# The SWA output and mix projections as one plain pair and three pairs of seven products

## The chip, the cores and the metric

The kernel runs on one core of one Trainium2 chip. The metric is the device time of one execution in microseconds (us). It is measured in several runs and given as their median; a profiled execution of the same program gives the durations of single instructions. Engines are named as the profile names them: PE is TensorE (matmuls), PEld its weight loads, DVE is VectorE, ACT is ScalarE, POOL is GpSimd, SP is SyncE, which issues nearly all DMAs here.

## What is computed

One step of a one-layer streaming encoder on 1024 prompt tokens and 64 sample tokens, 1088 columns in all, with a model width of 1024. The part that matters here merges two branches and adds the result to the input, after which cross-attention normalises it:

```python
def merge_branches(ret_o, ret_g, swa_o, gate_a, gate_b, w_ret_out, w_swa_out, w_mix_out):
    B, S = ret_g.shape[:2]
    a = (rms_norm(ret_o).astype(ret_g.dtype).reshape(B, S, -1) * jax.nn.silu(ret_g)) @ w_ret_out
    b = swa_o.reshape(B, S, -1) @ w_swa_out
    return (jax.nn.sigmoid(gate_a) * a + jax.nn.sigmoid(gate_b) * b) @ w_mix_out
...
x += merge_branches(...)
x += CrossAttn(RMSNorm(x), memory K/V)
x += SwiGLU(RMSNorm(x))
```

`w_swa_out` and `w_mix_out` are 1024 x 1024 each.

## The kernel before

Activations are kept transposed: feature rows on the 128 partitions (eight row tiles, k or m = 0 to 7), tokens along the free dimension. A full-precision product is made of three matmuls of rounded halves: `split` (line 122) copies a tile to a rounded high part on ACT and subtracts it on DVE for the low part, and high times high, high times low and low times high are summed in PSUM.

There are two ways to project. The dense way (`dense`, line 153) takes one weight tile row `m` against eight k and a chunk of 384, 384 or 320 columns (`CH`); `m_major` (line 1042) orders rows and chunks. The seven-product way (`strassen`, line 247) cuts a pair of weight rows, `m` and `m + 4`, and the activations into 2 x 2 quarters and makes seven products where a plain scheme (`plain`, line 225) makes eight. The quarters are 4 row tiles by half of the columns (`HALF` = 544, in two PSUM banks of 272), called B11, B12, B21 and B22, and the seven products need four differences of them, T1 to T4, as operands too. The weight sums are formed by four operations on POOL (`weight_ops`, line 166), and seven weight splits follow for a pair. Before the change the first projections, the FFN's gate and up and its down projection use seven products; the SWA output, the mix, the cross-attention and the retention output projections use the dense way.

SBUF holds two rings of eight large slots each (`Ring`, line 100), which stages take over from one another; a slot is written when its last reader is done. Scratch in DRAM (`d_swa`, `d_gate`, `d_mix`, `d_h`, `d_op`) carries results between stages. Pools hand out tiles in rotation, so a load waits for the buffer that it overwrites. PSUM has eight banks.

The stages around the change are these. `mix_phase` (line 843) runs the sliding-window attention; between its steps, PE gets pieces of the retention output projection (`filler`, line 1053), of which eight pieces remain after the last step, and whose gated results go to `d_mix`. The attention's tiles lie in ring 0, the retention operands in ring 1. At the end of `mix_phase` stands `merge_swa` (line 1101). It loads `d_swa` chunk by chunk, splits it into ring 0, projects with `w_swa_out`, multiplies by the gate (line 1121), adds `d_mix` (line 1122) and splits the result into ring 1, all on DVE and ACT. It then projects with `w_mix_out`, adds the input (line 1130), stores `d_h`, forms the gained and split operand `xc` of the next stage (`gained`, line 265) and sums the squares; as soon as a column chunk is complete its root is formed (`to_rstd`, line 309), through `later`, which runs after the next dense projection. `cross_phase` (line 1139) then projects `xc` with `w_cq`, in order of k, and scales by the roots.

The order of instructions on each engine is that of a scheduler which simulates the program by priorities; each engine and each DMA queue then runs its instructions in that order.

Of the kernel before, what the change touches and what calls it, by code (L numbers as in the profile page):

```python
# [109 lines left out]
class Kernel:  # L110
# [86 lines left out]
    def multiply(self, ps, w, xs, first=True, last=True):  # L197

        mm = self.nc.tensor.matmul
        for k, x in enumerate(xs):  # L200
            ks = slice(k * P, (k + 1) * P)
            start, stop = first and k == 0, last and k == len(xs) - 1
# [22 lines left out]
    def plain(self, w, x, emit, early=None):  # L225
# [19 lines left out]
        emit(1, 1, part(1, 1, 1), None)  # L245

# [86 lines left out]
    def run(self):  # L333
        nc, tc, io = self.nc, self.tc, self.io
        with ExitStack() as ctx:
# [34 lines left out]
            with ExitStack() as sctx:  # L370
# [472 lines left out]
    def mix_phase(self):  # L843
# [17 lines left out]
        self.merge_swa()  # L861
# [239 lines left out]
    def merge_swa(self):  # L1101
        nc, tc, io = self.nc, self.tc, self.io
        with ExitStack() as ctx:
            bp = ctx.enter_context(tc.tile_pool(name="bq", bufs=2, reuse_waits="tile"))
            pn = ctx.enter_context(tc.tile_pool(name="pnb", bufs=1, reuse_waits="tile", space=PSUM))
            self.norm_psum = lambda name: pn.tile([P, 512], F32, tag="n", name=name)
            ld = lambda: bp.tile([P, 384], F32, tag="ld", bufs=8, name="ld")
            unit = lambda w: [lambda m=m: self.unit(io[w][m], KT) for m in range(KT)]
            swas = self.ring_tiles(0, KT, "swa")
            for c0, n in CH:  # L1110
                for k in range(KT):
                    a = ld()
                    self.load(a[:, :n], self.d_swa[k, :, c0:c0 + n])
                    self.split(a[:, :n], swas[k][:, 0, c0:c0 + n], swas[k][:, 1, c0:c0 + n])
            mixs = self.ring_tiles(1, KT, "mix")
            for m, u, (c0, n) in self.m_major(unit("w_swa_out"), CH, lead=2):
                g, a = ld(), ld()
                self.load(g[:, :n], self.d_gate[2][m, :, c0:c0 + n])
                self.load(a[:, :n], self.d_mix[m, :, c0:c0 + n])
                ps = self.dense(u, swas, c0, n)  # L1120
                nc.vector.tensor_tensor(out=g[:, :n], in0=ps, in1=g[:, :n], op=ALU.mult)
                nc.vector.tensor_tensor(out=a[:, :n], in0=a[:, :n], in1=g[:, :n], op=ALU.add)
                self.split(a[:, :n], mixs[m][:, 0, c0:c0 + n], mixs[m][:, 1, c0:c0 + n])
            self.xs = self.ring_tiles(0, KT, "xc")
            for m, u, (c0, n) in self.m_major(unit("w_mix_out"), CH):
                x = ld()
                self.load(x[:, :n], io["xT"][m, :, c0:c0 + n])
                ps = self.dense(u, mixs, c0, n)
                x = x[:, :n]
                nc.vector.tensor_tensor(out=x, in0=ps, in1=x, op=ALU.add)  # L1130
                self.store(self.d_h[0][m, :, c0:c0 + n], x)
                acc = self.rstd[:, c0:c0 + n]
                self.gained(self.xs[m], c0, n, x, self.gains[:, 1, :], m)
                self.add_square(acc, x, m == 0, bp, n)
                if m == KT - 1:
                    root = self.root[:, c0 // 384, :]
                    self.later.append(lambda acc=acc, root=root: self.to_rstd(acc, acc, root=root))
# [559 lines left out]
```

## Time and profile before

| What | Value |
|---|---|
| median of 3 runs | 2241.72 us (2241.03 to 2244.38) |
| profiled execution, its own time | 2239.58 us |
| its span in the profile | 2237.8 us |
| SWA output projection in it | 1035.0 to 1130.5 us |
| mix projection in it | 1130.5 to 1227.2 us |
| mean granted PE clock | 0.986 |

Times in the profile count from the start of the span. A row of a group reads: line, engine, operation, output<-inputs by tile name, shapes, number of instructions, then busy time in us and mean ns of one, then idle time of the engine just before them and who ended it. A row of waits reads: the engine and instruction that waited, the one it waited for, then us in total, times, and the longest. A row of the timeline reads: start, duration, engine, line, operation.

### The profile page before, as it was taken

Reading aid. Unit: us, or ns where it says so; the run is one execution under the profiler, and the core shown is the slowest. Engines: PE = TensorE matmul, PEld = TensorE weight load, DVE = VectorE, ACT = ScalarE, POOL = GpSimd, SP = SyncE. Lnnn points to the kernel's source line nnn. Section 1 sums busy time; section 2 is a strip of 40 time slices with the busy share of each in tenths; the row PEclk is TensorE's granted clock in tenths of the full one; section 3 lists DMA queues with packets and bytes.
Section 4 is the critical chain, followed back from the end, with each engine's and each line's share of the span. In section 5 each row is a group of like instructions: output and inputs, shape, how many; then the busy total and the mean of one; then the engine's idle time right before and its main releaser. Section 6 shows DMA issues by size and latency. Waiting matters only on the chain.

```text
span 2237.8 us, 41757 instructions
## 1 busy us (share of the span) xinstructions
PE 2171.3 (97%) x16434; PEld 2106.8 (94%) x16434; DVE 1600.4 (72%) x2655; ACT 884.7 (40%) x1897; POOL 690.5 (31%) x466
## 2 busy tenths in 40 slices
PE   9999999999999989999999999999999999999996
PEld 9899999999999977779999998999999999999986
DVE  8986878676687668876455555668777777778588
ACT  7333333435444355553133333333222222334243
POOL 1441533342253112220000000014555555434462
PEclk9999999999999999999999999999999999999998
DMA  5433345443445475326443112422332332475233
GB/s 205 156 111 110 117 123 137 133 127 113 167 152 178 151 229 169 114 75 208 130 154 107 55 48 65 134 85 88 122 130 101 102 122 89 142 273 182 84 102 109
DMA packets 182599, 290.86 MB, mean 130 GB/s; under 512 B 40290, under 2 KB 110850, under 8 KB 182402
## 3 DMA queue, kind: packets, MB, share of 16 engines
q1 hardware_dynamic: 177794, 279.26, 39.3%
q10 hardware_dynamic: 4608, 8.91, 1.1%
q8 instruction: 130, 2.13, 0.4%
q14 instruction: 67, 0.55, 0.1%
HBM read 196.95 MB, written 91.16 MB: 129 GB/s over the span
## 4 chain that ended last, share of the span: by engine, by line
PE 75%; DVE 7%; DMA 4%; issue 1%; ACT 1%; POOL 1%; SPq 0%; DVEq 0%; ACTq 0%; POOLq 0%
PE pq L208 14%; PE pq L206 14%; PE pq L205 14%; PE pd L149 7%; PE pd L151 7%; PE pd L150 7%; PE pout L1000 1%; DMA hl<-d_op 1%; PE pp L984 1%; DVE wq L124 1%; PE pss L942 1%; DMA ld<-d_swa 1%; DVE B L124 1%; DMA raw<-w_ret_out 1%; PE pk L699 0%
## 5 line engine op out<-in xcount | busy, mean ns | idle before, releaser
L124 DVE TENSOR_TENSOR wq<-raw,wq 128x512 fp32r<-128x512 f32 (+1 forms) x505 | 450.1, 895 | 124.8 <-ACT wq L123 122.6
L123 ACT CAST wq<-raw 128x512 fp32r<-128x512 f32 (+1 forms) x505 | 307.6, 614 | 569.9 <-PE pq L208 262.7
L205 PE MATMUL pq<-T,wq 128*128 128x272 f32 x1832 | 493.9, 289 | 6.2 <-DVE u L252 3.6
L206 PE MATMUL pq<-T,wq 128*128 128x272 f32 x1832 | 493.9, 289 | 0.0
L206 PE MATMUL pq<-B,wq 128*128 128x272 f32 x1592 | 429.3, 289 | 8.4 <-DVE B L124 8.4
L205 PE MATMUL pq<-B,wq 128*128 128x272 f32 x1592 | 426.7, 288 | 0.0
L208 PE MATMUL pq<-T,wq 128*128 128x272 f32 x1832 | 384.4, 290 | 3.4 <-DVE wq L124 3.4
L183 POOL TENSOR_TENSOR raw<-raw 128x512 f32<-128x512 f32 (+1 forms) x59 | 79.4, 1345 | 894.8 <-DVE rs_r L291 483.8
L205 PEld LDWEIGHTS pq<-T,wq 128*128 128x128 f32 x1832 | 346.7, 189 | 7.1 <-DVE u L252 3.7
L206 PEld LDWEIGHTS pq<-T,wq 128*128 128x128 f32 x1832 | 346.8, 189 | 0.3 <-issue 0.3
L208 PE MATMUL pq<-B,wq 128*128 128x272 f32 x1592 | 334.0, 290 | 0.0
L206 PEld LDWEIGHTS pq<-B,wq 128*128 128x128 f32 x1592 | 300.7, 189 | 10.3 <-DVE B L124 10.0
L205 PEld LDWEIGHTS pq<-B,wq 128*128 128x128 f32 x1592 | 300.1, 189 | 0.7 <-issue 0.4
L208 PEld LDWEIGHTS pq<-T,wq 128*128 128x128 f32 x1832 | 292.0, 191 | 4.6 <-DVE wq L124 3.8
L208 PEld LDWEIGHTS pq<-B,wq 128*128 128x128 f32 x1592 | 253.5, 190 | 0.5 <-issue 0.3
L252 DVE TENSOR_TENSOR u<-pq,u 128x544 f32<-128x544 f32 x177 | 127.5, 720 | 111.7 <-PE pq L208 111.1
L186 POOL TENSOR_TENSOR raw<-raw 128x512 f32<-128x512 f32 (+1 forms) x59 | 85.3, 1446 | 125.2 <-DVE wq L124 122.6
L970 POOL TENSOR_TENSOR t<-t,den 128x768 f32<-128x768 f32 (+2 forms) x34 | 47.8, 1406 | 167.7 <-DVE den L968 49.9
L571 DVE TENSOR_TENSOR stage<-pq,u 128x544 f32<-128x544 f32 x112 | 80.3, 717 | 26.6 <-PE pq L208 25.8
L184 POOL TENSOR_TENSOR raw<-raw 128x512 f32<-128x512 f32 (+1 forms) x59 | 89.2, 1512 | 3.7
L1455 POOL TENSOR_TENSOR y<-u,y 128x544 f32<-128x544 f32 x38 | 62.6, 1658 | 72.4 <-DVE y L1453 54.4
L189 POOL TENSOR_TENSOR raw<-raw 128x512 f32<-128x512 f32 (+1 forms) x59 | 83.2, 1411 | 4.4
(373 smaller groups left out, 4674.2 us busy)
## 6 DMA issues: line engine op xcount, KB each, us to landing
hl<-d_op SPq DMA_DIRECT2D x85, 272.0 KB, 4.4
d_qkv<-stage SPq DMA_DIRECT2D x44, 272.0 KB, 2.3
d_op<-stage SPq DMA_DIRECT2D x44, 272.0 KB, 2.1
d_op<-ht SPq DMA_DIRECT2D x44, 272.0 KB, 3.3
raw<-w_gate SPq DMA_DIRECT2D x22, 512.0 KB, 3.5
raw<-w_up SPq DMA_DIRECT2D x22, 512.0 KB, 3.6
d_gate<-stage ACTq DMA_DIRECT2D x32, 272.0 KB, 2.8
raw<-w_down SPq DMA_DIRECT2D x16, 512.0 KB, 4.4
```

The lines of the kernel that those rows point to most:

```text
L123: self.last_cast = self.nc.scalar.copy(hi, src).ins
L124: return self.nc.vector.tensor_tensor(out=lo, in0=src, in1=hi.bitcast(F32), op=ALU.subtract).ins
L149: mm(ps, wh, xh, start=start, stop=False)
L150: mm(ps, wh, xl, start=False, stop=False)
L151: self.last_mm = mm(ps, wl, xh, start=False, stop=stop).ins
L184: tt(out=a21, in0=a21, in1=a22, op=add)
L186: tt(out=a11, in0=a22, in1=a11, op=sub)
L189: tt(out=a12, in0=a12, in1=a11, op=sub)
L205: mm(ps[:, c, :HC], w[:, 0, ks], x[:, 0, cs], start=start, stop=False)
L206: mm(ps[:, c, :HC], w[:, 0, ks], x[:, 1, cs], start=False, stop=False)
L208: self.last_mm = mm(ps[:, c, :HC], w[:, 1, ks], x[:, 0, c * HC:(c + 1) * HC], start=False, stop=stop).ins
L252: add = lambda out, a, b: nc.vector.tensor_tensor(out=out, in0=a, in1=b, op=ALU.add)
```

## The change

`merge_swa` is written anew, and it is called after `mix_phase` with PSUM to itself: `plain_psum` is closed before it and opened again, on the right side, for `cross_phase`; the memory tiles' pool is closed before it too.

- Both projections work on pairs of rows `n` and `n + 4`. Pair 0 is made plain (eight products, `quarters_in_parts`), pairs 1 to 3 with seven products each.
- The quarters of `d_swa` are loaded (16 tiles of 128 x 544) and split, the 16 differences T1 to T4 are formed in place on POOL and split. The slots are given by hand (`place`): B operands in ring 0, in the order in which the attention leaves its tiles, T operands in ring 1.
- The gated result of a pair is multiplied on DVE; the addition of `d_mix` is on POOL for pairs 0 to 2 and on DVE for pair 3; the differences of the results are formed on POOL. Most of them are stored to `d_op` and loaded again as the mix projection's operands: B12, B21 and B22 as the last pair's products free slots (`refill`), T1 to T4 after the first plain pair. Of B11 the pairs 1 and 2, and of all quarters pair 3, are split directly.
- In the mix projection's plain pair the products run over the first three k of all quarters, and then over the fourth.
- For pairs 1 to 3 of the mix projection the side sum is added to the input on POOL, and the PSUM part on DVE. `xc` is formed directly for pair 3; rows 0, 4, 1, 5, 2, 6 are loaded again from `d_h` as slots come free. The squares are summed per half of the columns.
- The roots of all three column chunks are formed through `later` in `cross_phase`, whose dense projections go over k in the order 0, 4, 1, 5, 2, 6, 3, 7.

```diff
-    def multiply(self, ps, w, xs, first=True, last=True):
+    def multiply(self, ps, w, xs, first=True, last=True, tiles=None):
...
+    def quarters_in_parts(self, w, x, emit, parts):
...
+        ps, left = {}, {}
+        for i, t, j, ks in parts:
+            left[i, t] = left.get((i, t), 0) + len(ks)
+        for i, t, j, ks in parts:
+            first = (i, t) not in ps
+            if first:
+                ps[i, t] = self.bank_pair()
+            left[i, t] -= len(ks)
+            out = self.multiply(ps[i, t], w[i, j], x[f"B{j + 1}{t + 1}"], first, not left[i, t], ks)
+            if not left[i, t]:
+                emit(i, t, out, None)
...
-                    with self.plain_psum():
+                    with self.plain_psum(side="right"):
                         self.mix_phase()
-                        self.mem.close()
+                    self.mem.close()
+                    self.merge_swa()
+                    with self.plain_psum(side="right"):
                         self.cross_phase()
...
+            self.fp = ctx.enter_context(tc.tile_pool(name="fm", bufs=1, reuse_waits="tile"))
+            left = ctx.enter_context(tc.tile_pool(name="ml", bufs=10, reuse_waits="tile"))
+            right = ctx.enter_context(tc.tile_pool(name="mr", bufs=8, reuse_waits="tile", side="right"))
+            self.ps = ctx.enter_context(tc.tile_pool(name="psm", bufs=4, reuse_waits="tile", space=PSUM))
...
+            for k in range(4):
+                b11, b12, b21, b22 = (raw[name, k] for name in ("B11", "B12", "B21", "B22"))
+                for out, x, y in ((b11, b12, b11), (b12, b22, b12), (b22, b22, b11), (b21, b21, b22)):
+                    nc.gpsimd.tensor_tensor(out=out, in0=x, in1=y, op=sub)
+                for name, x in (("T2", b22), ("T1", b11), ("T3", b12), ("T4", b21)):
+                    put(ops, name, k, x)
...
+                    g, a = fetch(self.d_gate[2][m, :, half(t)]), fetch(self.d_mix[m, :, half(t)])
+                    o = g
+                    if sb is None:
+                        tt(out=banks(o), in0=ps, in1=banks(g), op=ALU.mult)
+                    else:
+                        o = st()
+                        tt(out=banks(o), in0=ps, in1=sb, op=ALU.add)
+                        tt(out=o, in0=o, in1=g, op=ALU.mult)
+                    (nc.vector if last else nc.gpsimd).tensor_tensor(out=o, in0=o, in1=a, op=ALU.add)
+                    h[i, t], spare[i, t] = o, a
+                    name = quarter[i, t]
+                    if last or (name == "B11" and n):
+                        put(mixs, name, n, o)
+                    else:
+                        self.store(saved(name, n), o)
+                    for name, at, x, y in (("T1", (0, 0), (0, 1), (0, 0)), ("T2", (1, 1), (1, 1), "T1"),
+                                           ("T3", (0, 1), (1, 1), (0, 1)), ("T4", (1, 0), (1, 0), "T2")):
+                        if name not in h and x in h and y in h:
+                            h[name] = spare[at]
+                            nc.gpsimd.tensor_tensor(out=h[name], in0=h[x], in1=h[y], op=sub)
+                            self.store(saved(name, n), h[name])
...
+            self.quarters_in_parts(first, ops, gated(0), [(i, t, j, all4) for t in range(2) for j in range(2) for i in range(2)])
...
+            def refill(name):
+                new = {"B11": "B12", "B21": "B21", "T2": "B22"}.get(name)
+                if new:
+                    begin(mixs, places, new, place[name])
+                    for k in three:
+                        put(mixs, new, k, fetch(saved(new, k)))
...
+                    x = fetch(io["xT"][m, :, half(t)])
+                    if sb is not None:
+                        nc.gpsimd.tensor_tensor(out=banks(x), in0=banks(x), in1=sb, op=ALU.add)
+                    tt(out=banks(x), in0=ps, in1=banks(x), op=ALU.add)
+                    self.store(self.d_h[0][m, :, half(t)], x)
+                    if n == 3:
+                        gain(m, t, x)
...
+            for name, old in (("T2", "B22"), ("T1", "T1"), ("T3", "T3"), ("T4", "T4")):
+                begin(mixs, places, name, place[old])
+                for k in all4:
+                    put(mixs, name, k, fetch(saved(name, k)))
...
+            def norms(i=0):
+                c0, n = CH[i]
                 acc = self.rstd[:, c0:c0 + n]
...
+                self.to_rstd(acc, acc, root=self.root[:, i, :])
+                if i < 2:
+                    self.later.append(lambda: norms(i + 1))
...
+            order = (0, 4, 1, 5, 2, 6, 3, 7)
+            xs = [self.xs[k] for k in order]
```

More of the change, by code (lines that the diff above doesn't have):

```diff
@@ L1106, in merge_swa @@
[L1106 to L1123, printed above, removed]
@@ new lines, in fetch @@
+            def fetch(src):
+                a = st()
+                self.load(a, src)
+                return a
+            ring = lambda r, *slots: (r, [(self.rings[r].next + i) % KT for i in slots])
+            place = {"B11": ring(0, 5, 7), "B21": ring(0, 2, 1), "B12": ring(0, 0, 4), "B22": ring(0, 3, 6),
+                     "T1": ring(1, 0, 1), "T2": ring(1, 2, 3), "T3": ring(1, 4, 5), "T4": ring(1, 6, 7)}
+            pair = lambda w, n: self.load_raws([io[w][n], io[w][n + 4]])
+            saved = lambda name, k: self.d_op[OPS.index(name), k]
@@ L1172, in attend @@
                 for c0, n in CQ:
-                    ps = [self.dense(us[i], self.xs, c0, n) for i in range(2)]
+                    ps = [self.dense(us[i], xs, c0, n) for i in range(2)]
                     qf = t2("qf")
```

105 lines of the change are left out of this document (84 added, 21 removed).

## The prediction

> **What bounds the kernel now.** I read first the page's busy shares and its chain of waits.
>
> ```profile
> span 2237.8 us, 41757 instructions
> ...
> PE 2171.3 (97%) x16434; PEld 2106.8 (94%) x16434; DVE 1600.4 (72%) x2655; ACT 884.7 (40%) x1897; POOL 690.5 (31%) x466
> ...
> PE 75%; DVE 7%; DMA 4%; issue 1%; ACT 1%; POOL 1%; SPq 0%; DVEq 0%; ACTq 0%; POOLq 0%
> ```
>
> TensorE sets the end, so fewer matmuls shorten the kernel as long as nothing else in the stage takes over. Next, the view by stretches (columns: length, then busy time and instruction count of PE, PEld, DVE, ACT, POOL; clock; DMA share; GB/s): the two projections, then two stretches of the FFN, which already uses the seven-product form.
>
> ```profile
> 1035.00:1130.50 95.50, 95.29 (x579) 94.85 (x578) 54.04 (x102) 27.73 (x54) 0.00 (x0) 1.00 0.56 169
> 1130.50:1227.20 96.70, 96.70 (x596) 96.70 (x595) 48.84 (x98) 34.92 (x67) 0.00 (x0) 1.00 0.39 125
> 1600.00:1700.00 100.00, 100.00 (x805) 100.00 (x805) 72.75 (x88) 29.77 (x50) 55.43 (x38) 1.00 0.33 112
> 1920.00:2000.00 80.00, 78.27 (x627) 77.84 (x626) 63.55 (x86) 34.19 (x59) 26.60 (x17) 1.00 0.74 256
> ```
>
> The view of the tiles `swa` and `mix` puts the borders of the stages there:
>
> ```profile
> L149 PE MATMUL pd<-swa,wq x192: 306/334/442, 1035.2 to 1130.2; 128*128 128x384 f32 x128, 128*128 128x320 f32 x64
> L149 PE MATMUL pd<-mix,wq x192: 306/334/423, 1130.6 to 1226.9; 128*128 128x384 f32 x128, 128*128 128x320 f32 x64
> ```
>
> and TensorE's waits from 1015 to 1235 us are one:
>
> ```profile
> PE pd L149 <- ACT swa L123: 0.2, 1, 0.2
> ```
>
> So the old stage costs 95.5 + 96.7 = 192.2 us, all matmul, with GpSimd wholly idle and VectorE about half busy. A new loss there cannot replace an old wait: there is none.
>
> **Part 1, products removed.** In the FFN 805 matmuls of 272 columns take 100 us, 0.1242 us each; a product (4 k, 6 matmuls) is 24 of them, 2.98 us. The wide matmuls do 24 x 8 x 1088 columns in 95.5 us, 0.457 ns a column, and 272 of those are 0.1243 us: the narrow form loses nothing. Each projection goes from 32 products to 8 + 3 x 7 = 29: 86.4 us. Both: 192.2 - 172.8 = 19.4 us less PE work. The 1.2 us between the two stages is norm matmuls (596 instructions against 579) that only move behind the stage.
>
> **Part 2, what VectorE and GpSimd are given.** Prices, from the groups by form of 1035:1227 (first fence) and 1520:1920 (second), and the views of single lines (third: min/median/max ns):
>
> ```profile
> L124 DVE TENSOR_TENSOR wq<-raw,wq 128x512 fp32r<-128x512 f32 x33 | 22.8, 691 | 4.9 <-ACT wq L123 4.2
> ...
> L269 DVE SCALAR_TENSOR_TENSOR xc<-ld,gains,xc 128x384 fp32r<-128x384 f32 x16 | 9.9, 619 | 11.0 <-ACT xc L268 11.0
> ...
> L269 DVE SCALAR_TENSOR_TENSOR xc<-ld,gains,xc 128x320 fp32r<-128x320 f32 x7 | 3.8, 546 | 0.0
> ```
> ```profile
> L124 DVE TENSOR_TENSOR wq<-raw,wq 128x512 fp32r<-128x512 f32 x134 | 143.5, 1072 | 37.3 <-ACT wq L123 37.0
> ...
> L252 DVE TENSOR_TENSOR u<-pq,u 128x544 f32<-128x544 f32 x57 | 41.2, 723 | 48.6 <-PE pq L208 48.4
> ```
> ```profile
> L1388 POOL TENSOR_TENSOR ht<-stage x10: 1364/1372/1375, 1544.5 to 1919.6; 128x544 f32<-128x544 f32 x10
> ...
> L1388 DVE TENSOR_TENSOR ht<-stage x1: 716/716/716, 1977.4 to 1977.4; 128x544 f32<-128x544 f32 x1
> ```
> ```profile
> L183 POOL TENSOR_TENSOR raw<-raw x59: 1013/1295/2607, 20.4 to 2179.6; 128x512 f32<-128x512 f32 x55, 128x384 f32<-128x384 f32 x4
> ```
>
> The same weight split takes 691 ns while GpSimd is idle and 1072 where it works. The timeline of VectorE and of GpSimd around 1641 us says why:
>
> ```profile
> 1641.15 1.19 DVE L124 TENSOR_TENSOR wq<-raw,wq 128x512 fp32r<-128x512 f32 x1 [0.70 <-ACT wq L123]
> 1642.72 0.72 DVE L252 TENSOR_TENSOR u<-pq,u 128x544 f32<-128x544 f32 x1 [0.37 <-PE pq L208]
> ```
> ```profile
> 1640.43 1.37 POOL L1373 TENSOR_TENSOR stage<-stage,rstd_f 128x544 f32<-128x544 f32 x1
> 1641.75 1.75 POOL L184 TENSOR_TENSOR raw<-raw 128x512 f32<-128x512 f32 x1
> ```
>
> The split starts at 1641.15 and ends at 1642.34, 0.54 us after the GpSimd operation before it (1641.80): it waited and then ran. The GpSimd operation that starts meanwhile needs 1.75 us where 1.295 is usual: it waited for the split. The two take turns, with some 0.69 - 0.54 = 0.15 us of overlap per GpSimd operation. An add that reads PSUM (L252) runs beside GpSimd at its usual 0.72. The Trainium skill, page "SBUF — State Buffer", section "Who interferes with whom", calls this an exclusive lock between GpSimd and a VectorE operation with two SBUF inputs, one side fully blocked; the trace agrees but for that overlap, and without it the sum below would be some 11 us larger. It is a rule that speaks against this change.
>
> So I add what needs its turn. A VectorE operation with two SBUF inputs costs 0.717 (544 columns) or 0.691 (512), a gain 0.80 (0.619 plus 160 columns at the 73 ns per 64 between its two forms), GpSimd 1.364 or 1.295, less 0.14 per GpSimd operation.
>
> SWA projection, GpSimd: 16 differences of `swa`, 12 gated adds, 16 differences of `mix` (44 x 1.364 = 60.0) and 12 weight sums (15.5): 75.5. VectorE: 32 operand splits (22.9), 29 weight splits (20.0), 12 products by the gate and 4 last adds (11.5), 16 operand splits of `mix` (11.5): 66. Sum 141.5, less 56 x 0.14: 133.7 us.
>
> Mix projection, GpSimd: 12 weight sums and 12 adds, 31.9. VectorE: 16 splits of saved differences (11.5), 25 weight splits (17.3), 14 square sums (10.0), 16 gains (12.8): 51.6. Sum 83.5, less 24 x 0.14: 80.1 us.
>
> **Part 3, what of it is done early.** The last store of `d_swa`, and the last store out of the attention's spare buffers (tile view, SyncE's timeline):
>
> ```profile
> L120 SPq DMA_DIRECT2D d_swa<-osb x9: 370/371/386, 858.1 to 1020.4; - x9
> ```
> ```profile
> 1037.87 0.38 SPq L120 DMA_DIRECT2D d_mix<-swin  x1
> ```
>
> The first half's columns are stored well before, so B11 and B21 (8 splits, 5.7) and four weight splits (2.8) fit before 1035; of the second half, which loads after 1020.4, four B12 splits and four differences (2.9 + 4.9). B22's slots are those spare buffers, read until after 1038. Early: 16.3 us. Left: 133.7 - 16.3 + 80.1 = 197.5 us of turns against 172.8 of matmul. The turns, not TensorE, set this stage. All of it is needed: operands and weights by TensorE, adds and saved differences within a rotation of 18 buffers, so little of it can be put off; some 12 us of the first projection slip into the second, which is itself over (92 against 86.4). Bounds: 172.8, if turns cost nothing, to 197.5 / 0.88 = 224, if they are used only as far as the FFN does (16 GpSimd and 22 VectorE operations per 41.7 us pair, 36.6 us by these prices, 88%, with TensorE never waiting there). I take 197.5 + 3: queues in order, casts on ScalarE before each split, and a slower clock after a wait, as here:
>
> ```profile
> 1514.06 0.93 PE L330 MATMUL pb<-ident,rs_r 128*128 128x128 f32 x6 [2.05 <-ACT rstd_f L331]
> ...
> 1515.90 0.43 PE L206 MATMUL pq<-b,wq 128*128 128x272 f32 x1
> 1516.12 0.43 PE L205 MATMUL pq<-b,wq 128*128 128x272 f32 x1
> ...
> 1518.93 0.29 PE L206 MATMUL pq<-b,wq 128*128 128x272 f32 x1
> ```
>
> (0.22 us apart instead of 0.12 for 3 us, worth 1.4 us.)
>
> **Part 4, the end.** The norms now start after the last product: add 0.72, square 0.66, sum 0.72, then the steps that stand in the timeline before, pt to the root:
>
> ```profile
> 1221.68 0.72 PE L306 MATMUL pt<-ones,rstd 128*128 128x2 f32 x6
> ...
> 1224.43 0.15 DVE L294 SCALAR_TENSOR_TENSOR rs_r<-rs_t,rs_r 128x3 f32<-128x3 f32 x1
> ```
>
> 2.9, then spread and copy 1.3: about 6.3. TensorE has three projections of 256 columns to do meanwhile (24 x 0.117 = 2.8 each, three banks), and the order of k puts the last column tile last. Bounds 0 to 5, I take 2, plus the 1.2 of moved matmuls.
>
> **Part 5, DMA.** Quarter tiles are 272 KB (0.279 MB). First projection: about 10 `d_swa`, 32 gate and mix, 26 saves, 10 reloads, 8 weights: 26 MB, 270 to 300 GB/s over 86 to 97 us. All go through SyncE, where a load that waits for its buffer holds those behind it. The FFN's turn ran 256 GB/s at a share of 0.74, about 346 at full. I take 0; if the burst at the turn (last pair and next plain pair: 45 quarter tiles and 4 weights, 14.6 MB in 44.7 us) ran at 300, 4 us.
>
> **The sum.** 197.5 + 3 + 2 + 1.2 - 192.2 = +11.5 us. On the profiled execution (2239.6, span 2237.8) that is 2251.1; the median of the runs is 2.1 higher: 2253.
>
> **Rivals.**
> A. The turns are hidden. By engine alone the first projection needs 75.5 on GpSimd and 66 + 18 PSUM operations (12.9) = 79 on VectorE, both under 86.4. For it: in 1600:1700 both engines sum to 128 of 100 us while TensorE never waits. Against: that stage fills at most 88% of its time with turns, this one 114% (197.5 of 172.8). It needs early or put-off work of 25 us. Left are 2 at the start, the FFN's turn,
>
> ```profile
> PE pq L206 <- DVE B L124: 4.8, 5, 1.3
> ```
>
> and 3.2 at the end: -19.4 + 2 + 4.8 + 3.2 = -9.4, 2232.
> B. VectorE blocked by GpSimd frees PSUM late and TensorE's waits idle the turns again, so these are used only 88%: 224 + 3.2 - 192.2 = +35, 2277. It decides once the gated adds queue on GpSimd ahead of the next weights (12 GpSimd operations in the 20.9 us of a pair, 16 us at least). For: strict order on both. Against: four PSUM pairs give some slack.
> C. As A, with DMA late at the turn by 4 us: 2237.
>
> **How the numbers follow.** Forecast 0.50 (2245 to 2267), A 0.26, B 0.17, C 0.07. A run tells a change of 0.2%, 4.5 us. Faster: A, 0.26. Same: C and the low end of the forecast, 0.11. Slower: 0.63. For 8 in 10 the range takes in A and B: 2226 to 2281.
>
> **What would show it.** Matmuls of the stage about 1390 (two times 29 x 24) at 0.124; the stage lasting 197 to 205 us instead of 192; splits of `wq` there about 1.07 instead of 0.69 and GpSimd differences at 1.5 to 1.8; TensorE waiting for VectorE's operand and weight splits from the first seven-product pair on; the later stages unchanged. Wrong: TensorE without waits in the pairs, or long waits on loads.

## The result, and the profile after

The changed kernel takes 2277.13 us (median of 6 runs, 2275.40 to 2281.79) against 2241.49 us of the kernel before (6 runs beside it): a ratio of 1.0156, 95% interval 1.0143 to 1.0170. It is slower by 35.6 us, where 11.5 were forecast. The time lies inside the range, at its upper end, and nearest to rival B (2277).

The page of the profile after, the lines that stand against those of before:

```profile
span 2274.7 us, 42432 instructions
...
PE 2167.3 (95%) x16674; PEld 2100.4 (92%) x16674; DVE 1687.1 (74%) x2668; ACT 913.3 (40%) x1923; POOL 826.3 (36%) x546
...
PE 66%; DVE 10%; DMA 6%; issue 3%; POOL 2%; ACT 1%; SPq 0%; DVEq 0%; POOLq 0%; ACTq 0%
```

TensorE's work fell by 4 us, but its share of the chain fell from 75% to 66%; DVE, DMA and POOL took it. The view of TensorE's waits from 1018 to 1290 us, where before one wait of 0.2 us stood:

```profile
PE pd L149 <- DVE st L1232: 14.3, 1, 14.3
PE pq L206 <- DVE st L1232: 5.0, 3, 4.4
PE pq L207 <- DVE B L124: 4.4, 2, 4.1
PE pq L206 <- DVE u L268: 4.4, 1, 4.4
PE pq L206 <- ACT T L123: 3.7, 1, 3.7
PE pq L206 <- DVE st L1182: 3.0, 1, 3.0
PE pq L209 <- DVE wq L124: 1.7, 1, 1.7
PE pq L206 <- DVE st L1185: 1.1, 1, 1.1
PE pq L206 <- ACT u L271: 1.1, 2, 0.9
```

The wait of 14.3 us stands at the end of the stage, ahead of the first `w_cq` matmul; the others lie among the products and sum to 24.4 us. The view by stretches (columns as in the prediction) shows where:

```profile
1035.00:1060.00 25.00, 22.33 (x176) 22.11 (x175) 24.61 (x20) 14.21 (x24) 19.44 (x11) 1.00 0.43 157
1060.00:1085.00 25.00, 18.52 (x103) 17.69 (x104) 25.00 (x21) 7.20 (x13) 22.86 (x14) 0.73 0.38 119
1085.00:1110.00 25.00, 25.00 (x202) 25.00 (x202) 21.61 (x23) 5.74 (x11) 20.15 (x13) 1.00 0.75 237
...
1135.00:1147.40 12.40, 7.99 (x54) 7.77 (x53) 11.29 (x15) 4.85 (x9) 3.27 (x2) 0.86 0.99 344
...
1172.00:1197.00 25.00, 17.28 (x108) 17.06 (x109) 18.37 (x25) 14.10 (x23) 4.75 (x3) 0.80 0.69 243
1197.00:1222.00 25.00, 25.00 (x203) 25.00 (x202) 19.20 (x23) 7.71 (x13) 15.07 (x10) 1.00 0.55 191
...
1248.90:1263.20 14.30, 0.03 (x1) 0.06 (x1) 10.65 (x14) 6.52 (x11) 4.20 (x3) 0.62 0.61 198
```

The matmuls of the products carry their times in the trace, so each block of 24 gives one product; whatever it lasts beyond 2.98 us is its loss. The first matmul is at 1037.6, the first of `w_cq` at 1263.2: 225.6 us for the stage, against 192.2 before. Of this, 58 products are 172.8. The losses, with the products counted from 1:

| Where | Loss, us |
|---|---|
| products 7, 8 and 11 (end of the plain pair, start of the next) | 6.05 + 1.72 + 7.43 = 15.2 |
| products 24, 25, 27 and 28 (last SWA pair) | 1.39 + 0.29 + 0.43 + 6.00 = 8.1 |
| products 38 and 40 (turn from the mix projection's plain pair to the next) | 6.74 + 5.23 = 12.0 |
| products 54, 55 and 58 | 2.4 |
| the wait ahead of the first `w_cq` matmul | 14.3 |

They sum to 52.0; the last 0.8 us is spread. The products' losses (37.7) are larger than their waits (24.4), mostly because TensorE runs at half pace after a long wait. After the first one:

```profile
1061.41 0.60 PE L207 MATMUL pq<-B,wq 128*128 128x272 f32 x1 [4.08 <-DVE B L124]
1061.80 0.43 PE L206 MATMUL pq<-B,wq 128*128 128x272 f32 x1
...
1067.51 0.43 PE L206 MATMUL pq<-B,wq 128*128 128x272 f32 x1
...
1068.52 0.29 PE L206 MATMUL pq<-B,wq 128*128 128x272 f32 x1
```

Matmuls start 0.23 us apart until about 1067.9 and 0.13 apart from there: 6.5 us at half pace, some 3.3 us lost behind a wait of 4.1. The change of the whole span, 36.9 us, is 33.4 of the stage, 2.6 by which the stage starts later, and 0.9 of all the rest. Among the profiles of this study the start lies anywhere from 1032.9 to 1040.1, so the 2.6 say little about the change.

### The profile page after: what moved, and what is told of

It reads as the page before. It is cut to its first block, busy times and chain, and to the rows that moved or that the text cites. A ratio compares the mean times of both kernels' runs of the same rounds, so it can differ in the third digit from the quotient of the medians.

```text
span 2274.7 us, 42432 instructions
## 1 busy us (share of the span) xinstructions
PE 2167.3 (95%) x16674; PEld 2100.4 (92%) x16674; DVE 1687.1 (74%) x2668; ACT 913.3 (40%) x1923; POOL 826.3 (36%) x546
## 4 chain that ended last, share of the span: by engine, by line
PE 66%; DVE 10%; DMA 6%; issue 3%; POOL 2%; ACT 1%; SPq 0%; DVEq 0%; POOLq 0%; ACTq 0%
PE pq L209 14%; PE pq L206 14%; PE pq L207 14%; PE pd L149 5%; PE pd L150 5%; PE pd L151 4%; DVE wq L124 2%; DVE T L124 2%; PE pout L1017 1%; DMA hl<-d_op 1%; PE pp L1001 1%; DVE B L124 1%; PE pss L959 1%; DMA st<-d_op 1%; DMA raw<-w_ret_out 1%
## 5 line engine op out<-in xcount | busy, mean ns | idle before, releaser
L124 DVE TENSOR_TENSOR wq<-raw,wq 128x512 fp32r<-128x512 f32 (+1 forms) x523 | 483.6, 931 | 134.6 <-ACT wq L123 132.4
L206 PE MATMUL pq<-T,wq 128*128 128x272 f32 x2024 | 546.7, 290 | 15.4 <-ACT T L123 3.7
L123 ACT CAST wq<-raw 128x512 fp32r<-128x512 f32 (+1 forms) x523 | 316.3, 614 | 578.8 <-PE pq L209 233.3
L207 PE MATMUL pq<-T,wq 128*128 128x272 f32 x2024 | 546.0, 289 | 0.0
L207 PE MATMUL pq<-B,wq 128*128 128x272 f32 x1864 | 504.2, 290 | 13.0 <-DVE B L124 13.0
L206 PE MATMUL pq<-B,wq 128*128 128x272 f32 x1864 | 502.1, 289 | 10.1 <-DVE u L268 4.4
L209 PE MATMUL pq<-T,wq 128*128 128x272 f32 x2024 | 425.2, 290 | 5.1 <-DVE wq L124 5.1
L206 PEld LDWEIGHTS pq<-T,wq 128*128 128x128 f32 x2024 | 383.7, 190 | 18.2 <-ACT wq L123 6.2
L209 PE MATMUL pq<-B,wq 128*128 128x272 f32 x1864 | 391.7, 290 | 0.0
L207 PEld LDWEIGHTS pq<-T,wq 128*128 128x128 f32 x2024 | 383.5, 189 | 0.3 <-issue 0.3
L207 PEld LDWEIGHTS pq<-B,wq 128*128 128x128 f32 x1864 | 353.7, 190 | 15.4 <-DVE B L124 15.1
L206 PEld LDWEIGHTS pq<-B,wq 128*128 128x128 f32 x1864 | 353.5, 190 | 11.6 <-DVE u L268 4.6
L183 POOL TENSOR_TENSOR raw<-raw 128x512 f32<-128x512 f32 (+1 forms) x65 | 92.5, 1424 | 712.9 <-DVE rs_r L307 270.2
L209 PEld LDWEIGHTS pq<-T,wq 128*128 128x128 f32 x2024 | 322.9, 191 | 6.6 <-DVE wq L124 5.8
L209 PEld LDWEIGHTS pq<-B,wq 128*128 128x128 f32 x1864 | 297.6, 191 | 0.5 <-issue 0.3
L268 DVE TENSOR_TENSOR u<-pq,u 128x544 f32<-128x544 f32 x195 | 140.1, 719 | 105.3 <-PE pq L209 104.4
L186 POOL TENSOR_TENSOR raw<-raw 128x512 f32<-128x512 f32 (+1 forms) x65 | 94.0, 1446 | 139.8 <-DVE wq L124 137.3
L184 POOL TENSOR_TENSOR raw<-raw 128x512 f32<-128x512 f32 (+1 forms) x65 | 97.2, 1495 | 3.9
L189 POOL TENSOR_TENSOR raw<-raw 128x512 f32<-128x512 f32 (+1 forms) x65 | 93.0, 1431 | 4.6
L149 PE MATMUL pd<-xc,wq 128*128 128x256 f32 (+1 forms) x256 | 76.0, 297 | 14.3 <-DVE st L1232 14.3
```

Of the source, the lines that this page charges most:

```text
L123: self.last_cast = self.nc.scalar.copy(hi, src).ins
L124: return self.nc.vector.tensor_tensor(out=lo, in0=src, in1=hi.bitcast(F32), op=ALU.subtract).ins
L149: mm(ps, wh, xh, start=start, stop=False)
L183: tt(out=a11, in0=a11, in1=a21, op=sub)
L184: tt(out=a21, in0=a21, in1=a22, op=add)
L186: tt(out=a11, in0=a22, in1=a11, op=sub)
```

## The experiments

Theory: the losses are separate queues in order. At the start VectorE and GpSimd, in turns, have more to do than the first eleven products last; at 38 and 40 the operands' way through scratch is late; at the end the order of loads on SyncE is. First rival: one cause, the turns between the two engines, feeds all of them. Second rival: a DMA that is too slow. The table holds all kernels that ran, with the losses read as above ("start": products 7 to 12; "SWA": the rest up to product 31; "turn": up to 42 in kernels with seven products in both projections; "mix": the rest of the mix projection; "end": the wait of the first `w_cq` products for their columns). A sum is read to within 0.5 us. The kernel before took between 2239.9 and 2242.5 us beside them. The kernel e5_all_dve of an expectation is 10 here.

| Kernel | Median us | Ratio to before, 95% | start | SWA | turn | mix | end |
|---|---|---|---|---|---|---|---|
| changed kernel | 2277.1 | 1.0156 (1.0143 to 1.0170) | 15.2 | 8.1 | 12.0 | 2.4 | 14.3 |
| 1 differences on VectorE | 2274.6 | 1.0142 (1.0092 to 1.0192) | 10.8 | 5.6 | 12.2 | 2.4 | 16.0 |
| 2 no differences | 2259.1 | 1.0077 (1.0047 to 1.0108) | 1.1 | 4.8 | 11.7 | 1.8 | 14.6 |
| 3 xT loads ahead | 2267.1 | 1.0108 (1.0059 to 1.0157) | 14.9 | 8.0 | 11.7 | 0 | 8.9 |
| 4 no reload | 2266.4 | 1.0105 (1.0069 to 1.0141) | 17.2 | 6.5 | 1.2 | 7.3 | 13.1 |
| 5 all three of 2, 3, 4 | 2246.3 | 1.0021 (1.0010 to 1.0032) | 0.9 | 7.2 | 1.0 | 3.1 | 7.4 |
| 6 earlier loads | 2277.2 | 1.0155 (1.0126 to 1.0185) | 15.4 | 8.0 | 11.9 | 1.7 | 14.5 |
| 7 SWA projection plain | 2259.4 | 1.0077 (1.0054 to 1.0100) | 0 | 0 | | 6.3 | 22.2 |
| 8 mix projection plain | 2248.1 | 1.0019 (1.0002 to 1.0037) | 14.8 | 1.9 | | 0 | 0.9 |
| 9 as 7, xT loads ahead | 2251.2 | 1.0047 (1.0032 to 1.0062) | 0 | 0 | | 4.8 | 7.8 |
| 10 all differences and sums of the mix on VectorE | 2256.1 | 1.0070 (1.0054 to 1.0085) | 8.8 | 6.5 | 8.1 | 0 | 3.8 |
| 11 nothing on GpSimd | 2253.5 | 1.0051 (1.0035 to 1.0068) | 4.9 | 2.8 | 8.5 | 0 | 0.4 |
| 12 two plain SWA pairs, mix plain | 2232.0 | 0.9965 (0.9952 to 0.9979) | 0 | 0 | | 0 | 0 |

**1. The 16 SWA differences on VectorE.**

```diff
-                    nc.gpsimd.tensor_tensor(out=out, in0=x, in1=y, op=sub)
+                    nc.vector.tensor_tensor(out=out, in0=x, in1=y, op=sub)
```

> The 16 differences of the SWA operands go from GpSimd to VectorE, all else as in the changed kernel. Theory of turns: a pair of operations that take turns costs about 1.8 us, 16 GpSimd differences of 1.78 us are replaced by 16 VectorE operations of 0.72, so some 17 us of turns leave the first 60 us of the stage. TensorE's waits in the seventh and eleventh product (7.7 and 7.4 us with the slow clock after them) shrink to 5 us or less together: about 2267. Rival, that the waits come from late slots or loads of the second half: both waits stay, within 3 us of 2277.

It took 2274.6 (its two executions: 2271.0 and 2278.2). The loss at products 7 and 8 is gone, that at 11 is larger (10.8 with the next one, against 7.4): moving this work alone changes whom it delays, and neither expectation holds in full: the time is within 3 us of 2277, but not both waits stay. The splits of the differences last 1102 ns instead of 1603, but VectorE is busy without a gap from 1045 to 1085.

**2. Those differences left out; T is split from the raw quarters.**

```diff
-                for out, x, y in ((b11, b12, b11), (b12, b22, b12), (b22, b22, b11), (b21, b21, b22)):
-                    nc.gpsimd.tensor_tensor(out=out, in0=x, in1=y, op=sub)
```

> Leaves out the 16 differences of the SWA operands: T1 to T4 are split from the raw quarters. Theory of turns: as in the run with the differences on VectorE, and 11 us of VectorE work less; the waits of the seventh and eleventh product nearly vanish, 2262 to 2265. Rival, late slots: the seventh product's 6 to 8 us stay, 2270 or more.

It took 2259.1, 18.0 less, and the start loses 1.1 instead of 15.2; the other places change by 3.3 us at most. So the volume ahead of product 11 is the cause of the start's loss, and not of theirs.

**3. The xT tiles of pairs 1 to 3 loaded ahead of the pair's weights.**

```diff
+                ahead = {(i, t): fetch(io["xT"][n + 4 * i, :, half(t)]) for i, t in ((0, 0), (1, 1), (0, 1), (1, 0))}
                 w = self.weight_ops(pair("w_mix_out", n))
```

> The four input tiles that the pairs 1 to 3 of the mix projection add are loaded ahead of the pair's weights instead of each at its result. Theory: the 14.3 us that TensorE waits before the cross-attention's first products is one input load that SyncE issues only behind the store of the result before it, 5 us before it is used; loaded ahead, the wait falls to under 3 us and the time by 11 to 15 us, to 2262 to 2266. Rival, that VectorE's and ScalarE's gains at the end (16 of 0.8 us) are what is late: the wait stays over 8 us, 2270 or more.

In the changed kernel the end looks so, on SyncE, GpSimd and VectorE in three views of the timeline:

```profile
1256.20 0.33 SPq L120 DMA_DIRECT2D d_h<-st  x1
1256.58 0.42 SPq L117 DMA_DIRECT2D st<-xT  x1
```
```profile
1260.93 1.33 POOL L1231 TENSOR_TENSOR st<-st,u 128x544 f32<-128x544 f32 x1 [6.59 <-DMA st<-xT]
```
```profile
1262.30 0.72 DVE L1232 TENSOR_TENSOR st<-pq,st 128x544 f32<-128x544 f32 x1 [3.47 <-POOL st L1231]
```

The last xT tile is asked for 7.7 us after the last product, behind a store that waits for a result itself; GpSimd waits for it, VectorE for GpSimd, and `w_cq` for the column. With the loads ahead the wait falls to 8.9, not below 3, and the time to 2267.1 (2263.6 and 2270.5). So the order of loads is a part of the wait, and a part stays, as in the rival. That it stands in VectorE's own queue is read from the timeline and not tested by itself: in this run, two gains (0.77 us each elsewhere) are held up by two GpSimd adds from 1240.8 to 1244.4, and a split by a third:

```profile
1241.29 3.66 DVE L285 SCALAR_TENSOR_TENSOR xc<-st,gains,xc 128x544 fp32r<-128x544 f32 x2
...
1246.20 1.81 DVE L124 TENSOR_TENSOR wq<-raw,wq 128x512 fp32r<-128x512 f32 x1
...
1250.50 0.71 DVE L1232 TENSOR_TENSOR st<-pq,st 128x544 f32<-128x544 f32 x1
```

**4. The saves to `d_op` and their loads left out; a constant tile takes the operands' place (one buffer fewer).**

```diff
-                        put(mixs, new, k, fetch(saved(new, k)))
+                        put(mixs, new, k, still)
...
-                    put(mixs, name, k, fetch(saved(name, k)))
+                    put(mixs, name, k, still)
```

> Leaves out the stores of the gated results and differences to DRAM scratch and their loads (26 of each); the operands are split from one constant tile, so VectorE's and ScalarE's work is the same; the rotation has 17 buffers instead of 18. Theory that the losses at the turn between the projections (6.5 us in product 27, 6.7 in product 38, 5.4 in product 40) come from the burst of DMA and from VectorE's queue standing behind splits that wait for loads: products 38 and 40 lose nothing, 12 us less, 2265; product 27, which I put down to turns with GpSimd, stays. Rival, that all three are turns: all stay, 2275 to 2279. If all are DMA: 18 us less, 2259.

It took 2266.4. The turn loses 1.2 instead of 12.0, so this was the way through scratch; 2.0 us more at the start and 4.9 more in the mix take a part of it back. Product 28 (27 in the expectation) loses 5.2 though the burst of loads is gone: what delays it in the changed kernel isn't DMA, although the stretch before it moved 344 GB/s at a share of 0.99.

**5. Edits 2, 3 and 4 together.**

> Leaves out together what the single runs left out (the SWA differences; the stores to and loads from scratch) and loads the inputs ahead. If the three causes are separate, the savings add: 2277 less about 15, 12 and 6, 2244, with product 28 (6 us) and the end (8) as what is left. If they hide each other, under 2236; if one cause sits behind all, no better than 2255.

It took 2246.3: 30.8 us less than the changed kernel, where the three edits one by one sum to 18.0 + 10.1 + 10.8 = 38.9. These are medians of two or three executions that lie up to 7 us apart; the losses in the table, which leave out where the stage starts, fall by 18.0 + 8.5 + 6.7 = 33.2 one by one and by 32.4 together. The three places are separate; what is left, 7.2 about product 28 and 7.4 at the end, none of them touches.

**6. `d_swa` as two tensors, one for each half of the columns, so that a load of the first half doesn't stand behind the last store.**

```diff
-            self.d_swa = dp.tile([KT, P, T], F32, name="d_swa")
+            self.d_swa = [dp.tile([KT, P, HALF], F32, name=f"d_swa{i}") for i in range(2)]
```

> The attention's result lies in two scratch tensors, one for each half of the columns, so the first half's quarters need not be loaded behind the last store. Theory: 8 loads and splits move from 1026 to 1038 us to before that, which is the part of my 16 us of early work that did not come early; VectorE has 15 us idle there. The losses of the seventh to eleventh product fall from 15 us to 5 to 9: 2268 to 2272. Rival, that the loads stay behind something else on SyncE: no change, 2275 or more.

It took 2277.2, a miss. SyncE's timeline in the changed kernel, and in this one:

```profile
1025.43 0.33 SPq L117 DMA_DIRECT2D raw<-w_swa_out  x1
1025.86 0.38 SPq L117 DMA_DIRECT2D st<-d_swa  x1
```
```profile
1027.32 0.33 SPq L117 DMA_DIRECT2D raw<-w_swa_out  x1
1027.75 0.38 SPq L117 DMA_DIRECT2D st<-d_swa  x1
```

In both the loads follow a weight load that waited for its buffer. Moving that load behind them wasn't tried.

**7. The SWA projection in four plain pairs**, the mix projection as changed; the loads in program order, the two rings exchanged.

```diff
-            for n in range(1, 4):
-                w = self.weight_ops(pair("w_swa_out", n))
-                self.refill = refill if n == 3 else None
-                self.strassen(w, ops, gated(n))
+            for n in range(4):
+                w = self.plain_weights(pair("w_swa_out", n)) if n else first
+                self.quarters_in_parts(w, ops, gated(n), [(i, t, j, all4) for t in range(2) for j in range(2) for i in range(2)])
```

> Only the mix projection keeps pairs of seven products; the SWA projection is four plain pairs, so its differences and GpSimd weight sums are gone and the four quarters of its result are split directly into the free ring (loads in program order, the rings change places for the stages after). Theory: the first 60 us lose nothing more (15 us less), nor does the turn's product 28, at the price of 9 us of matmul; the wait of 14 us for the late input load at the end stays: 2277 - 21 + 9 = 2265 if products 38 and 40 lose their 12 us still (saved differences are still loaded), 2254 if these came from the burst of reloads. Rival, that the losses only move later: 2270 or more.

It took 2259.4. The mix products lose 6.3 in place of 14.4, and the SWA part nothing; the end waits 22.2 us.

**8. The mix projection in four plain pairs**, the SWA projection as changed; the columns `xc` formed where the results appear, nothing reloaded, loads in program order.

```diff
-                w = self.weight_ops(pair("w_mix_out", n))
-                self.refill = to_columns if n == 3 else None
-                self.strassen(w, mixs, mixed(n))
+                w = self.plain_weights(pair("w_mix_out", n))
+                self.quarters_in_parts(w, mixs, mixed(n), [(i, t, j, all4) for t in range(2) for j in range(2) for i in range(2)])
```

> Only the SWA projection keeps pairs of seven products; the mix projection is four plain pairs without differences, and the columns of the next stage are formed from each result directly, none loaded again. Theory: the first 60 us lose 15 us as in the changed kernel, product 28 up to 6; 38 and 40 and the end lose nothing but 3; 9 us more matmul: 2277 - 12 - 11 + 9 = 2263. If the saved differences on GpSimd were what blocked product 28, 2257. Rival, that the late loads are SyncE's order in general: the end still waits over 8 us, 2270.

It took 2248.1, better than expected: with the mix's losses the end went too, to 0.9, and product 28 loses nothing. No differences of results are formed beside it there, and fewer results are reloaded; which of the two does it wasn't separated. The start is as in the changed kernel (14.8), and it eats more than the 8.9 us of the three products saved.

**9. As 7, with the xT loads ahead.**

> SWA projection in four plain pairs, mix projection as in the changed kernel with seven products in three pairs, and the xT tiles of pairs 1 to 3 loaded ahead of each pair's weights. Theory (the 22 us at the end of the run with the plain SWA projection are SyncE's order): the wait at the end falls to 7 to 10 us, 2244 to 2249. Rival (the end is VectorE's queue whatever the loads do): the wait stays above 15 us, above 2253.

It took 2251.2. The wait at the end falls from 22.2 to 7.8 as expected; the time came out 2 us above the upper bound expected from that, and no lower than before the change.

**10. The differences of `swa` and of the results, and the mix's sums, on VectorE.** The expectation speaks of every GpSimd operation; in this kernel the gated adds and the weight sums stayed on GpSimd.

```diff
-                            nc.gpsimd.tensor_tensor(out=h[name], in0=h[x], in1=h[y], op=sub)
+                            nc.vector.tensor_tensor(out=h[name], in0=h[x], in1=h[y], op=sub)
...
-                        nc.gpsimd.tensor_tensor(out=banks(x), in0=banks(x), in1=sb, op=ALU.add)
+                        nc.vector.tensor_tensor(out=banks(x), in0=banks(x), in1=sb, op=ALU.add)
```

> The changed kernel with every GpSimd operation of the two projections (differences, gated adds, weight sums, adds of the sum tile) on VectorE. Theory (the two engines take turns, so GpSimd's help is worth little): as with the 16 differences alone on VectorE the start still loses about 11 us, splits stay at 0.7 us, the later waits for reloads and the end stay: 2268 to 2277. Rival (GpSimd carries real load and VectorE alone becomes the bound in the whole of both projections): above 2285.

It took 2256.1, far below both: the theory that GpSimd's help is worth nothing was too kind to it. The gain lies where edit 1 had none: product 38 loses nothing (6.7 before), the mix nothing, the end 3.8 (a wait of 6.7 for the roots follows). SyncE's timeline at the turn, changed kernel first, fits that:

```profile
1153.34 4.07 SPq L117 DMA_DIRECT2D st<-d_op  x2
1162.59 2.12 SPq L120 DMA_DIRECT2D d_op<-st  x2
1164.76 2.55 SPq L117 DMA_DIRECT2D st<-d_op  x4
```
```profile
1150.00 0.95 SPq L120 DMA_DIRECT2D d_op<-st  x2
1151.27 2.36 SPq L117 DMA_DIRECT2D st<-d_op  x3
1153.72 0.38 SPq L120 DMA_DIRECT2D d_op<-st  x1
```

With the differences on GpSimd, SyncE stands until 1162.6 for two saves, and the loads of T behind them stand too. GpSimd was late with these differences because a weight sum ahead of them, 1.3 us alone, took 5.50 us while VectorE went from one operation with two SBUF inputs to the next:

```profile
1155.26 5.50 POOL L183 TENSOR_TENSOR raw<-raw 128x512 f32<-128x512 f32 x1 [16.91 <-DVE wq L124]
```

On VectorE the same saves go out from 1150.0.

**11. The gated adds and the weight sums on VectorE as well** (to edit 10).

```diff
-        tt = nc.gpsimd.tensor_tensor
+        tt = (nc.vector if vec else nc.gpsimd).tensor_tensor
...
-                    (nc.vector if last else nc.gpsimd).tensor_tensor(out=o, in0=o, in1=a, op=ALU.add)
+                    nc.vector.tensor_tensor(out=o, in0=o, in1=a, op=ALU.add)
```

> The kernel of e5_all_dve left the gated adds and the weight sums on GpSimd (36 operations); here these too are on VectorE, and GpSimd has nothing in the two projections. Theory (GpSimd's help costs as much as it brings, since the two engines take turns and its results come late): VectorE gets 36 operations of 0.7 us, 25 us, and its splits fall back to 0.7 us everywhere; it had some 50 us free in the 200 of the stage, so the time stays within 5 us of the 2256 before it, 2251 to 2261, and the start still loses 8 to 13 us. Rival (what was won came from the saved differences alone, and VectorE is now the bound in the SWA half): above 2264, with losses in every pair of the SWA half.

It took 2253.5, 23.6 less than the changed kernel and inside what the theory gave, with a start that loses less than expected (4.9); the rival falls. All 80 operations that GpSimd had are now on VectorE, yet VectorE is busy for less time. Up to the last sum of squares, so that both stretches hold the same work, changed kernel first:

```profile
1037.60:1265.30 227.70, 188.85 (x1404) 185.72 (x1403) 187.49 (x207) 87.91 (x146) 134.50 (x80) 0.91 0.61 207
```
```profile
1034.40:1239.50 205.10, 184.83 (x1428) 182.68 (x1427) 183.47 (x287) 87.56 (x146) 0.00 (x0) 0.95 0.66 230
```

And its splits from 1036 to 1237 us, in the same order:

```profile
L124 DVE TENSOR_TENSOR wq<-raw,wq 128x512 fp32r<-128x512 f32 x46 | 50.3, 1110 | 11.6 <-ACT wq L123 11.4
L124 DVE TENSOR_TENSOR T<-st,T 128x544 fp32r<-128x544 f32 x32 | 36.5, 1166 | 12.1 <-ACT T L123 12.1
```
```profile
L124 DVE TENSOR_TENSOR wq<-raw,wq 128x512 fp32r<-128x512 f32 x52 | 35.1, 688 | 6.5 <-ACT wq L123 6.5
L124 DVE TENSOR_TENSOR T<-st,T 128x544 fp32r<-128x544 f32 x32 | 22.6, 725 | 5.3 <-ACT T L123 5.3
```

So GpSimd's part in the loss is 23.6 of 35.6 us, and the first rival, the turns as one cause, is right for that part at most.

Product 28 loses nothing here, but 6.0 with edit 10. In the changed kernel VectorE's queue delays it: four splits of 1.8 us each, beside a gated add and four differences on GpSimd, stand ahead of the add that frees PSUM (L268):

```profile
1131.73 3.68 DVE L124 TENSOR_TENSOR B<-st,B 128x544 fp32r<-128x544 f32 x2
1135.33 3.57 DVE L124 TENSOR_TENSOR wq<-raw,wq 128x512 fp32r<-128x512 f32 x2
1138.82 0.71 DVE L124 TENSOR_TENSOR B<-st,B 128x544 fp32r<-128x544 f32 x1
1139.45 0.71 DVE L268 TENSOR_TENSOR u<-pq,u 128x544 f32<-128x544 f32 x1
```

With edit 10 the same loss looks different: GpSimd is idle then, and VectorE stands idle for 1.89 us ahead of that add, in front of a split whose reload from `d_op` has not landed. What makes up the rest there stays open:

```profile
1129.56 0.72 DVE L124 TENSOR_TENSOR B<-st,B 128x544 fp32r<-128x544 f32 x1 [1.89 <-ACT B L123]
```

**12. Two plain SWA pairs, then two of seven products; the mix plain as in 8.** The SWA differences, on VectorE, are spread over the results of the two plain pairs, and the gated adds of these two pairs are on VectorE; the loads are in program order, as in 7 and 8.

```diff
+            steps = [None, (("T1", "T3", "T2"), (0, 1), ("T1",)), (("T1", "T3", "T2"), (2, 3), ("T1",)),
+                     (("T4",), (0, 1), ("T4",)), (("T4",), (2, 3), ("T4",)), ((), (0, 1), ("T3",)),
+                     ((), (2, 3), ("T3",)), ((), (0, 1), ("T2",)), ((), (2, 3), ("T2",))]
...
+                    step = steps.pop(0) if steps else None
+                    if step:
+                        form(*step)
```

> Mix projection plain (four plain pairs, columns formed where the results appear, nothing through d_op for it), SWA projection with two plain pairs first and only the last two pairs with seven products; the 16 differences and the sums of the first two pairs on VectorE, each difference formed after one of the first two pairs' results instead of all before the first. Theory (the loss of 15 us at the start is too much VectorE and GpSimd work before product 11; with a second plain pair the operands of differences are needed 24 us later): 30 + 32 products, 184.8 us of matmul; the start loses under 5 us, so the stage lasts 186 to 192 us and the kernel 2233 to 2240. Rival (the seven-product pairs bring the waits with them wherever they stand): the loss of about 15 us moves to products 18 to 22, and the time stays near the 2248 of the kernel with three seven-product pairs, less nothing.

It took 2231.99 us against 2239.91 of the kernel before beside it, a ratio of 0.9965 (0.9952 to 0.9979): faster than both kernels. The stage:

```profile
1033.33:1218.52 185.19, 185.19 (x1491) 185.19 (x1490) 128.82 (x185) 68.23 (x113) 16.86 (x12) 1.00 0.55 185
```

62 products at 2.98 are 184.8; it lasts 185.2, with TensorE busy throughout at full clock. It saves only two products, but no time is lost between them. Which of its changes against experiment 8 does this (the second plain pair, the spreading, or VectorE in GpSimd's place) wasn't separated.

## Why the prediction was right or wrong

**What bounds the kernel, and Part 1: right.** Where nothing waits, the products last what was said: 25.00 of 25 us in two stretches after, and 185.2 for 62 in experiment 12. The rest of the program moved by 0.9 us.

**Part 2, the turns: right in kind, and in price at the start.** Weight splits were to last 1.07 us and lasted 1.11; differences on GpSimd were to last 1.5 to 1.8 and lasted 1.78, as the groups from 1036 to 1086 us show:

```profile
L1168 POOL TENSOR_TENSOR st<-st 128x544 f32<-128x544 f32 x16 | 28.2, 1781 | 27.2 <-DVE B L124 26.4 <-POOL st L1168 0.7
L124 DVE TENSOR_TENSOR T<-st,T 128x544 fp32r<-128x544 f32 x16 | 25.1, 1603 | 0.0
```

Experiment 11 takes the turns away and the splits are back at 0.69 and 0.73. The Trainium skill, page "SBUF — State Buffer", section "Who interferes with whom", has the exclusive lock; these rows agree with it. But in the prediction an operation waits for one operation of the other engine at most. The weight sum of 5.50 us at 1155.26 waited for a run of them, and in experiment 10 one took 9.25.

**The steps that failed: Part 4's 2 us for the end and Part 5's 0 for DMA.** The forecast for the stage was 197.5 + 3 + 2 = 202.5 us; it took 225.6, 23.1 more. The end lost 14.3 (12.3 more than its term) and the turn through scratch 12.0: 24.3. What Part 3 foresaw, 197.5 + 3 - 172.8 = 27.7 us lost among the products, came to 15.2 + 8.1 + 2.4 = 25.7.

**Part 3, "197.5 + 3", one volume of turns spread over the stage: near in number, wrong as a picture.** That the number is near is in part luck, since three things in it were off.

First, the 16.3 us of early work. Before the first product only these operand splits ran:

```profile
1030.81 0.73 DVE L124 TENSOR_TENSOR B<-st,B 128x544 fp32r<-128x544 f32 x1 [3.65 <-ACT B L123]
...
1031.92 2.10 DVE L124 TENSOR_TENSOR B<-st,B 128x544 fp32r<-128x544 f32 x3
1035.39 0.73 DVE L124 TENSOR_TENSOR B<-st,B 128x544 fp32r<-128x544 f32 x1 [1.36 <-ACT B L123]
...
1036.50 0.72 DVE L124 TENSOR_TENSOR B<-st,B 128x544 fp32r<-128x544 f32 x1
```

Six operand splits (4.3 at the prices of Part 2) and the weight splits (at most 2.8) are 7.1. The prediction let the first half's loads go early and dated the second half's by the last store of `d_swa`; all 16 stood on SyncE behind that store and a weight load. The other 9 us met the start, where the two engines were full already; with 7.1 in place of 16.3 the sum would have said 36.9 lost among the products, not 27.7. That these 9 explain the 15.2 lost there wasn't shown, since experiment 6 failed to bring the loads forward; that the volume at this place does, experiment 2 shows, and 12 agrees.

Second, the volume isn't spread. Five places lose 52.0 us, and between them VectorE and GpSimd have idle time that nothing can use (1197 to 1222: TensorE never waits). A sum over the stage can't see a place.

Third, the slow clock after each wait was taken as part of 3 us; the products lost 37.7 with 24.4 of waits, so it was most of 13.3.

**Part 4, the end: wrong.** It was taken at 2, bounds 0 to 5, for the norms. The wait was 14.3 and stood earlier, at the columns. The step left out SyncE's order, in which an xT load stands behind a store that waits (experiment 3: 5.4 of it), and the gains and `w_cq` splits queued on VectorE beside GpSimd (most of the rest goes in experiments 10 and 11, where waits of 6.7 for the roots and, in 11, of 3.0 for columns and 5.2 for the squares then appear behind the first `w_cq` matmul).

**Part 5, DMA: wrong in kind.** It was taken at 0, bound 4, by rate. The rate was as foreseen at its highest, 344 GB/s, and harmless (experiment 4); the 12.0 us at the turn came at 243 GB/s, from a chain of difference, save and load through one queue. Experiment 10 removes product 38's part of it by making the saves early; the part at 40 grows from 5.2 to 8.1.

**The rivals.** A and C fell: they needed hidden turns. B gave 224 for the turns and 2277 in all; its mechanism, late frees of PSUM behind VectorE's blocked queue, is right for products 11, 24 and 28; at 38 the add that frees PSUM stood behind splits that waited for reloads, 6.55 us at once. Experiment 11 gives 23.6 us as the price of GpSimd in this stage. But B's number is chance: it has neither the reload nor the end, and its 88% leaves out the 0.14 us of overlap that the other sums take off. With it the FFN's pair holds 34.4 of 41.7 us, 83%, the turns come to 239 and B to 2292. What is left after experiment 11, 11 us over before, isn't due to turns.

## What to carry to other kernels

A stage that another stage hands over to must be costed at its start, its turn and its end, each with what is queued on every engine and on the issuing queue at that point; a sum of work over the stage is only a lower bound. Fewer matmuls pay only as far as their operands are ready: here two plain pairs first, and the differences formed between their results, gained 8 us where the fuller version lost 36. In this stage work given to GpSimd wasn't free beside VectorE's many operations with two SBUF inputs, so try the version with VectorE alone.

## What the runs showed of the hardware

GpSimd's 80 operations, 134.5 us of its time, made VectorE's busy time 4.0 us longer (187.5 against 183.5) than doing these 80 operations as well: a GpSimd difference lasts 1.36 alone, VectorE does it in 0.72, and beside GpSimd a split of VectorE lasts 1.11 to 1.17 in place of 0.69 to 0.73. The two engines need not alternate one by one: a GpSimd sum of 1.3 us took 5.50 and, in experiment 10, 9.25 us while VectorE had operations in a row.

Long waits cost TensorE more than themselves: behind a wait of 4.1 us the matmuls ran at half pace for 6.5 us, and every wait of 3.0 us or more among the products of these kernels was followed by half pace within some eight matmuls. Lone shorter waits were not: behind one of 1.15 us (product 24 of the changed kernel) and one of 2.44 us (experiment 11) the matmuls followed 0.12 to 0.15 us apart once the first had run:

```profile
1092.69 0.39 PE L206 MATMUL pq<-T,wq 128*128 128x272 f32 x1 [2.44 <-ACT wq L123]
```

The Trainium skill, page "TensorE: Matmul & The Clock Gate", section "Why this matters for your kernels", warns of gaps above about 3 us; these traces agree. The wait of 2.05 us quoted in the prediction, with 3 us at half pace behind it, doesn't speak against it: a second wait of 0.52 us follows it, with only six narrow matmuls between the two.
